# The first feed-forward of a mixer block begun row tile by row tile on four pairs of output blocks, in eight PSUM banks, with GpSimd taken out of the opening

## The chip, the cores and the metric

One NeuronCore of a Trainium2 chip runs the whole program. The metric is the device time of one execution in microseconds, lower being better; a verdict compares several executions of two kernels on the same chip.

## The reference

The block has a sequence of 512 rows and a width of 1024. A vector `c` gives nine modulation vectors of 1024 through one large matrix; the first feed-forward, the subject here, uses the first three (shift, scale, gate).

```python
cs  = silu(c)                                      # 1 x 1024
mod = (cs @ w_ada + b_ada).reshape(1, 3, 3, 1024)  # w_ada: 1024 x 9216
h   = rms_norm(x, norm_ffn1) * (1 + mod[:, 0, 1]) + mod[:, 0, 0]
gate, up = split(h @ w_ffn1_in, 2)                 # w_ffn1_in: 1024 x 5632
x   = x + 0.5 * mod[:, 0, 2] * ((silu(gate) * up) @ w_ffn1_out)
...                                                # token mixer, second feed-forward, final norm
```

All arrays are fp32.

## The kernel before, in words

Activations are held transposed: eight row tiles of 128 features by 512 sequence positions (`x[:, k]`, k = 0 to 7). A product in near-fp32 precision is made of three matmuls on fp32r operands: each operand is split into a rounded part and a remainder (`hh`/`hl` for the activations, `whi`/`wlo` for the weights), and `mm3` adds whi·hh, whi·hl and wlo·hh for every row tile k into one PSUM bank of 128 x 512. ScalarE makes the rounded part (a Copy, L226 for weights, L320 for activations), VectorE or GpSimd the remainder by a subtraction (L227, L321).

The opening, before the first feed-forward can run freely, goes so. SyncE loads `c` as one row, then `x`, `cols`, two constant matrices, and then the modulation matrix in 1 MB pieces (`adaw`, five buffers) and the first weights (`raw`, two buffers). `c` goes through Silu and is spread over the 128 partitions as `cs` by matmuls against a row of ones and two PSUM copies (L246 to L251). ScalarE squares the tiles of `x` (L291), VectorE adds them (L293), TensorE sums over partitions, GpSimd takes the power -0.5 (L308), TensorE spreads the result into a bank and ScalarE copies it to `rbs` (L405).

Then a loop over q = 0 to 3 (L409 to L418) takes two row tiles at a time: `ada(1, q)` and `ada(0, q)` compute scale and shift of tiles 2q and 2q + 1 by VectorE multiply-and-accumulate instructions (L260, 128 x 1024 each, four in a round); for q < 2 the weights of one pair of output blocks (gate and up block j = q, 1 MB) are split, with the remainder on GpSimd; GpSimd multiplies `x[:, k]` by `rbs` (L415), ScalarE applies scale and shift (L416) and rounds (L320), VectorE makes the remainder (L321).

`ffn` has 22 pairs of output blocks in two halves of 11, and an output product of eight blocks behind each half. Its first two pairs use four banks (`big`, `big`, `st`, `st`), the following ones the three `big` banks in turn; each pair is 48 matmuls, and then ScalarE and VectorE compute silu(gate)·up and split it. Beside it run 28 pieces of the remaining modulation work (`side`, 1 MB and two L260 instructions each), the first behind pair 2; their buffers lie where the opening's pool `p0` was.

Instructions are written in program order, but a planner sets the order on each engine and each queue from its own estimates of when operands and buffers are ready: an instruction whose inputs come late by the estimate is passed by later ones. Each engine then runs its list strictly in that order.

Of the kernel before, what the change touches and what calls it, by code (L numbers as in the profile page):

```python
# [17 lines left out]
P = 128  # L18
# [4 lines left out]
DFF = 2816  # L23
NJ = DFF // P
HJ = NJ // 2
H = 8
EPS = 1e-6
QS = float(P) ** -0.5
# [60 lines left out]
def layout(inputs):  # L89
    g = {k: np.asarray(v) for k, v in inputs.items()}  # L90

    def col(v):
        return v.reshape(-1, P).T

    def ktile(w):
        return w.reshape(-1, P, w.shape[1]).transpose(1, 0, 2)

    a = {}
    a["xT"] = ktile(g["x"][0].T)
    a["wada"] = g["w_ada"][0].T.reshape(36, 2, P, D).transpose(0, 2, 1, 3)  # L100
    a["crow"] = g["c"]
    cw = g["gdn_conv_w"][0].reshape(5, 24, P).transpose(2, 1, 0).reshape(P, 120)
    a["cols"] = np.concatenate([
        col(g["b_ada"][0]), col(g["norm_ffn1"][0]), col(g["norm_mix"][0]),
        col(g["norm_ffn2"][0]), col(g["norm_final"]), cw,
        col(g["mlstm_out_norm"][0]), col(g["gdn_out_norm"][0])], axis=1)
    mb, dt = g["mlstm_gate_bias"][0], g["gdn_dt_bias"][0]
    z = np.zeros(8, mb.dtype)
    a["rows"] = g["gdn_a_log"][0].reshape(1, 16)
    a["gbias"] = np.concatenate([mb[1], mb[3], dt[0], dt[1], mb[0], mb[2], z, z])[:, None]  # L110
    for n in (1, 2):
        wi = g[f"w_ffn{n}_in"][0].reshape(KO, P, 2, NJ, P)
        a[f"wi{n}"] = wi.transpose(3, 1, 0, 2, 4)
        wo = g[f"w_ffn{n}_out"][0].reshape(2, HJ, P, KO, P)
        a[f"wo{n}"] = wo.transpose(3, 0, 2, 1, 4)
    wk = ktile(g["w_in"][0])

    def blk(base, i):
        return wk[:, :, base + i * P: base + (i + 1) * P]

    def pair(b0, i0, b1, i1):
        return np.concatenate([blk(b0, i0), blk(b1, i1)], axis=2)

    gi = [MG + 8, MG + 24, GG, GG + 16, MG, MG + 16, GG + 8, GG + 24]
    a["wgate"] = np.concatenate([wk[:, :, b:b + 8] for b in gi] + [np.zeros((P, KO, 64), wk.dtype)], axis=2)
    a["wmqk"] = np.stack([pair(MQ, h, MK, h) for h in range(H)])
    a["wmv"] = np.stack([wk[:, 4 * kp:4 * kp + 4, MV + 512 * n: MV + 512 * (n + 1)]
                         for n in range(2) for kp in range(2)])
    a["wgkq"] = np.stack([pair(GK, h, GQ, h) for h in range(H)])
    for nm, b in (("wmo", MO), ("wgv", GV), ("wgz", GZ), ("wmm", MM), ("wmg", MGG)):  # L130
        a[nm] = np.stack([wk[:, :, b + 256 * i: b + 256 * (i + 1)] for i in range(4)])
    for nm, k in (("wbm", "w_branch_mlstm"), ("wbg", "w_branch_gdn"), ("wout", "w_out")):
        w = ktile(g[k][0])
        a[nm] = np.stack([w[:, :, 256 * i: 256 * (i + 1)] for i in range(4)])
    a["cst"] = _constants()
    return {k: np.ascontiguousarray(v) for k, v in a.items()}
# [25 lines left out]
def hybrid_block(ctx: ExitStack, tc: tile.TileContext, I, outT, dbg=None, upto=99):  # L162
# [21 lines left out]
    def sm():  # L184
        b = ps.tile([P, S], F32, tag="sm", name="psm", bufs=3)
        return b

    def mm(o, l, r, start=True, stop=True):
        pe.matmul(o, l, r, start=start, stop=stop)  # L189
# [7 lines left out]
    p0s = ExitStack()  # L197
    cs = p1.tile([P, D], F32, name="cs")
    p0 = Lines(p0s.enter_context(tc.tile_pool(name="p0", bufs=1, side="right")))
    crow = p0.tile([1, D], F32, name="crow")  # L200
    nc.sync.dma_start(crow, I["crow"])
    cstt = cst.tile([P, NK], F32, name="cstt")
    for q in range(4):
        nc.sync.dma_start(x[:, q * 2:(q + 1) * 2], I["xT"][:, q * 2:(q + 1) * 2])
    nc.sync.dma_start(cols, I["cols"])
    nc.sync.dma_start(cstt[:, 0:2 * P], I["cst"][:, 0:2 * P])
    C = {n: cstt[:, i * P:(i + 1) * P] for i, n in enumerate(KEPT)}
    one1 = C["ones"][:, 0:1]

    def colv(n):  # L210
        o, w = COL_OFF[n]
        return cols[:, o:o + w]
# [17 lines left out]
    def wk(src, c=256, lo=vec):  # L230
        hi, lo = wtile(src, KO * c, lo)
        return (hi[:, :KO * c].rearrange("p (k c) -> p k c", c=c),
                lo[:, :KO * c].rearrange("p (k c) -> p k c", c=c))
# [8 lines left out]
    modc = cst.tile([P, 72], F32, name="modc")  # L242
    scol = cst.tile([P, 24], F32, name="scol")
    ghalf = cst.tile([P, 16], F32, name="ghalf")
    orow = p0.tile([1, P], F32, name="orow")
    vec.memset(orow, 1.0)  # L246
    act.activation(crow, crow, AF.Silu)
    for q in range(2):
        pcs = sm()
        mm(pcs, orow, crow[:, q * S:(q + 1) * S])  # L250
        vec.tensor_copy(cs[:, q * S:(q + 1) * S], pcs)  # L251
    nrm = {0: "n1", 1: "nm", 2: "n2"}

    def ada(bk, q, tp, nb=2):
# [64 lines left out]
    def split(dst_h, dst_l, src):  # L319
        act.activation(dst_h, src, AF.Copy)  # L320
        vec.tensor_tensor(out=dst_l, in0=src, in1=dst_h.bitcast(F32), op=ALU.subtract)  # L321
# [20 lines left out]
    def ffn(x, hh, hl, gcol, wi, wo, tp, norm, side=(), pre=(), first=(ALL,), store=None):  # L342
        side, pre = list(side), list(pre)
        sq = {}
        for half in range(2):
            ah, al = [], []
            for jj in range(HJ):
                j = half * HJ + jj
                if j == 0:
                    w0 = pre or [wk(wi[i]) for i in range(2)]  # L350
                    p0 = [(big(), big()), (st2(), st2())]
                    for c, _ in first:
                        for (wh, wl), pp in zip(w0, p0):
                            for o, c0 in zip(pp, (0, P)):
                                mm3(o[:, c], lambda k: wh[:, k, c0:c0 + P], lambda k: wl[:, k, c0:c0 + P],
                                    lambda k: hh[:, k, c], lambda k: hl[:, k, c])
                if j < 2:
                    pg, pu = p0[j]
                else:
                    wh, wl = wk(wi[j])  # L360
                    pg, pu = big(), big()
                    for o, c0 in ((pg, 0), (pu, P)):
                        mm3(o, lambda k: wh[:, k, c0:c0 + P], lambda k: wl[:, k, c0:c0 + P],
                            lambda k: hh[:, k], lambda k: hl[:, k])
                sg = tp.tile([P, S], F32, tag="sg", name="sg", bufs=2)
                act.activation(sg, pg, AF.Silu)  # L366
                vec.tensor_tensor(out=sg, in0=sg, in1=pu, op=ALU.mult)  # L367
                a_h = tp.tile([P, S], F32R, tag="acth", name="acth", bufs=HJ + 2)
                a_l = tp.tile([P, S], F32R, tag="actl", name="actl", bufs=HJ + 2)
                split(a_h, a_l, sg)  # L370
                ah.append(a_h)
                al.append(a_l)
                if side and j > 1:
                    side.pop(0)()

            def out_block(o, wh, wl, c):
                po = big()
                mm3(po[:, c], lambda k: wh[:, k * P:(k + 1) * P], lambda k: wl[:, k * P:(k + 1) * P],
                    lambda k: ah[k][:, c], lambda k: al[k][:, c], n=HJ)
                vec.scalar_tensor_tensor(out=x[:, o, c], in0=po[:, c], scalar=gcol[:, o:o + 1], in1=x[:, o, c],  # L380
                                         op0=ALU.mult, op1=ALU.add)
                if half == 1:
                    sumsq(x, o, sq, tp, c)
                    if store is not None and c.stop == S:
                        nc.sync.dma_start(store[:, o], x[:, o])

            for o in range(KO - 2 * half):
                out_block(o, *wtile(wo[o, half], HJ * P), ALL[0])
                if half == 0 and side:
                    side.pop(0)()  # L390
        w2 = [wtile(wo[o, 1], HJ * P) for o in (KO - 2, KO - 1)]
        for c, ts in HALVES:
            for o, w in zip((KO - 2, KO - 1), w2):
                out_block(o, *w, c)
            norm(sq, c, ts)
        assert not side, len(side)
# [7 lines left out]
    rbs = p0.tile([P, S], F32, name="rbs")  # L404
    act.activation(rbs, rb, AF.Copy)  # L405
    hh, hl = new_h()
    pre = []
    for q in range(4):
        ada(1, q, p0, 5)  # L409
        ada(0, q, p0, 5)  # L410
        if q < 2:
            pre.append(wk(I["wi1"][q], lo=pool))
        for k in range(2 * q, 2 * q + 2):
            xn = p0.tile([P, S], F32, tag="xn", name="xn", bufs=4)
            pool.tensor_tensor(out=xn, in0=x[:, k], in1=rbs, op=ALU.mult)  # L415
            act.activation(xn, xn, AF.Identity, bias=modc[:, k:k + 1], scale=scol[:, k:k + 1])  # L416
            split(hh[:, k], hl[:, k], xn)
    p0s.close()  # L418
    pa1 = Lines(p1s.enter_context(tc.tile_pool(name="pa1", bufs=1, side="right")))
    gbias = cst.tile([64, 1], F32, name="gbias")  # L420
# [856 lines left out]
```

## Time and profile before

| | us |
|---|---|
| median of 3 runs | 1614.32 (1611.21, 1614.32, 1614.54) |
| the profiled execution | 1608.13 |
| its span, first to last instruction | 1606.3 |
| TensorE, granted clock over the span | 0.991 |

Engine names: PE is TensorE (PEld its weight loads), DVE VectorE, ACT ScalarE, POOL GpSimd, SP the queue that issues the DMAs. In a timeline row the first number is the start, the second the time to the end of the group of `xN` instructions; in brackets stands the idle time before it and what ended that. Durations of matmuls overlap, so the distance between starts is what one costs.

### The profile page before, as it was taken

The numbers are of one execution on the slowest core, as the hardware profiler recorded it, in microseconds if no ns is written. First come the engines' busy times: TensorE is split into PE (matmuls) and PEld (weight loads), VectorE is DVE, ScalarE is ACT, GpSimd is POOL, SyncE is SP. The second block draws the span as 40 slices with busy tenths as digits, with TensorE's granted clock in tenths as the row PEclk, the third lists the DMA queues.
The fourth block names the chain that finished last, engine by engine and source line by source line (L and its number), as shares of the span: only waits on it lengthen the run. The fifth ranks groups of instructions, "written<-read, shape, count | busy, mean of one in ns | idle before, by whom it ended". The sixth has DMA issues, their size and how long they took to land.

```text
span 1606.3 us, 20850 instructions
## 1 busy us (share of the span) xinstructions
PE 1553.8 (97%) x7944; PEld 1296.2 (81%) x7944; DVE 879.3 (55%) x1625; ACT 686.6 (43%) x1538; POOL 117.7 (7%) x121
## 2 busy tenths in 40 slices
PE   3999999999999999999999998999999999999997
PEld 2788888888878888888888886888889888888887
DVE  6878753333855555566666689346656433333333
ACT  3322122222526767595685732247623322123232
POOL 4100000000000000012111203500000000000000
PEclk9999999999999999999999998999999999999999
DMA  8577742223311111344544495676352222332122
GB/s 336 198 301 261 281 169 102 97 79 126 142 69 63 53 53 54 111 154 148 209 181 148 170 323 150 209 246 240 127 182 80 101 83 73 121 108 97 71 90 71
DMA packets 68613, 236.04 MB, mean 147 GB/s; under 512 B 23201, under 2 KB 25633, under 8 KB 50466
## 3 DMA queue, kind: packets, MB, share of 16 engines
q1 hardware_dynamic: 68514, 234.72, 41.2%
q8 instruction: 63, 1.03, 0.2%
q14 instruction: 36, 0.29, 0.1%
HBM read 199.04 MB, written 35.65 MB: 146 GB/s over the span
## 4 chain that ended last, share of the span: by engine, by line
PE 86%; DVE 8%; DMA 2%; ACT 1%; issue 1%; SPq 0%; POOL 0%; POOLq 0%; DVEq 0%; ACTq 0%
PE pbig L189 72%; PE pst L189 7%; PE psm L189 7%; DVE adaw L260 1%; DVE ot L1009 1%; DVE Wm L1011 1%; DVE wlo L227 1%; DMA vt<-vtd 1%; DVE hl L321 1%; PE pst L837 0%; DMA X<-xtd 0%; ACT whi L226 0%; DVE sqacc L293 0%; DMA raw<-in_wi 0%; PE pst L870 0%
## 5 line engine op out<-in xcount | busy, mean ns | idle before, releaser
L189 PE MATMUL pbig<-hh,whi 128*128 128x512 f32 (+1 forms) x1328 | 522.2, 394 | 8.4 <-ACT hh L320 8.4
L189 PE MATMUL pbig<-hh,wlo 128*128 128x512 f32 (+1 forms) x1328 | 519.5, 391 | 1.4 <-POOL wlo L227 1.4
L189 PE MATMUL pbig<-hl,whi 128*128 128x512 f32 (+1 forms) x1328 | 518.4, 391 | 2.5 <-DVE hl L321 2.4
L226 ACT ACTIVATE whi<-raw 128x1024 fp32r<-128x1024 f32 (+1 forms) x257 | 245.5, 991 | 461.9 <-PE pbig L189 388.0
L227 DVE TENSOR_TENSOR wlo<-raw,whi 128x1024 fp32r<-128x1024 f32 (+1 forms) x253 | 283.8, 1142 | 50.2 <-ACT whi L226 44.8
L189 PEld LDWEIGHTS pbig<-hh,whi 128*128 128x128 f32 x1328 | 251.1, 189 | 57.7 <-ACT hh L320 9.5
L189 PEld LDWEIGHTS pbig<-hl,whi 128*128 128x128 f32 x1328 | 251.2, 189 | 52.8 <-DVE hl L321 4.1
L189 PEld LDWEIGHTS pbig<-hh,wlo 128*128 128x128 f32 x1328 | 250.9, 189 | 51.3 <-POOL wlo L227 1.9
L367 DVE TENSOR_TENSOR sg<-sg,pbig 128x512 f32<-128x512 f32 x42 | 28.8, 687 | 245.5 <-PE pbig L189 245.5
L189 PE MATMUL pbig<-acth,whi 128*128 128x512 f32 (+1 forms) x396 | 146.1, 369 | 0.0
L189 PE MATMUL pbig<-acth,wlo 128*128 128x512 f32 (+1 forms) x396 | 145.6, 368 | 0.0
L189 PE MATMUL pbig<-actl,whi 128*128 128x512 f32 (+1 forms) x396 | 145.6, 368 | 0.0
L260 DVE SCALAR_TENSOR_TENSOR adaw<-adaw,cs 128x1024 f32<-128x1024 f32 x72 | 91.3, 1293 | 12.4 <-DMA adaw<-in_wada 12.3
L189 PEld LDWEIGHTS pbig<-acth,whi 128*128 128x128 f32 x396 | 74.5, 188 | 13.1
L189 PEld LDWEIGHTS pbig<-acth,wlo 128*128 128x128 f32 x396 | 74.5, 188 | 13.1
L189 PEld LDWEIGHTS pbig<-actl,whi 128*128 128x128 f32 x396 | 74.5, 188 | 13.0
L380 DVE SCALAR_TENSOR_TENSOR x<-pbig,ghalf,x 128x512 f32<-128x512 f32 (+1 forms) x36 | 24.8, 690 | 107.4 <-PE pbig L189 107.4
L830 DVE SCALAR_TENSOR_TENSOR cacc<-pbig,cols,cacc 128x510 f32<-128x510 f32 (+1 forms) x96 | 69.9, 745 | 24.5 <-ACT cacc L825 23.1
L366 ACT ACTIVATE sg<-pbig 128x512 f32<-128x512 f32 x42 | 25.1, 598 | 132.1 <-PE pbig L189 132.1
L308 POOL TENSOR_TENSOR rr<-ms,mhalf 128x2 f32<-128x2 f32 (+1 forms) x7 | 6.1, 876 | 928.3 <-DVE ms L305 734.9
L885 POOL TENSOR_SCALAR kd<-tt,ckd 128x128 f32<-128x128 f32 x64 | 46.0, 740 | 240.2 <-DVE ckd L881 156.6
L701 DVE TENSOR_TENSOR bd<-psm,negm 128x512 f32<-128x512 f32 x16 | 10.3, 685 | 38.8 <-PE psm L189 38.8
(338 smaller groups left out, 1985.5 us busy)
## 6 DMA issues: line engine op xcount, KB each, us to landing
raw<-in_wi SPq DMA_DIRECT2D x44, 1024.0 KB, 4.8
adaw<-in_wada SPq DMA_DIRECT2D x36, 1024.0 KB, 6.8
raw<-in_wo SPq DMA_DIRECT2D x32, 704.0 KB, 4.1
raw<-in_wmqk SPq DMA_DIRECT2D x8, 1024.0 KB, 4.8
raw<-in_wgkq SPq DMA_DIRECT2D x8, 1024.0 KB, 5.6
tad<-TA SPq DMA_DIRECT2D x8, 1024.0 KB, 4.5
raw<-in_wmv SPq DMA_DIRECT2D x4, 1024.0 KB, 4.8
raw<-in_wmo SPq DMA_DIRECT2D x4, 1024.0 KB, 4.8
```

The source lines that it names most:

```text
L189: pe.matmul(o, l, r, start=start, stop=stop)
L226: act.activation(hi[:, e], raw[:, e], AF.Copy)
L227: lo.tensor_tensor(out=wl[:, e], in0=raw[:, e], in1=hi[:, e].bitcast(F32), op=ALU.subtract)
L260: vec.scalar_tensor_tensor(out=raw[:, n], in0=raw[:, n], scalar=1.0, in1=cs, op0=ALU.mult, op1=ALU.mult, accum_out=acc[:, n:n + 1])
L321: vec.tensor_tensor(out=dst_l, in0=src, in1=dst_h.bitcast(F32), op=ALU.subtract)
L366: act.activation(sg, pg, AF.Silu)
L367: vec.tensor_tensor(out=sg, in0=sg, in1=pu, op=ALU.mult)
L380: vec.scalar_tensor_tensor(out=x[:, o, c], in0=po[:, c], scalar=gcol[:, o:o + 1], in1=x[:, o, c], op0=ALU.mult, op1=ALU.add)
L830: vec.scalar_tensor_tensor(out=acc[:, o], in0=pz[:, i], scalar=w[:, j:j + 1], in1=acc[:, o], op0=ALU.mult, op1=ALU.add)
L885: pool.tensor_scalar(out=kd[:, d, t], in0=ktt[:, t], scalar1=ckd[:, t, d, h:h + 1], scalar2=None, op0=ALU.mult)
L1009: vec.tensor_tensor(out=ov, in0=Um[:, d, r, j:j + 1].to_broadcast([P, n, 32 - n]), in1=Wm[:, d, j:j + 1, c].to_broadcast([P, n, 32 - n]), ...
L1011: vec.tensor_tensor(out=Wm[:, d, r, c], in0=Wm[:, d, r, c], in1=ov, op=ALU.subtract)
```

## The change

`c` is loaded by one DMA into all 128 partitions and goes through Silu there; the matmuls and copies that spread it are gone. The constants are loaded ahead of `cols`. The weights of the first four pairs are laid out anew on the way in (`wis`: for every row tile, the four pairs' gate and up columns, 0.5 MB a tile), and the loop runs over the eight row tiles: load scale and shift pieces (0.5 MB each) and the weights of the tile, split the weights (remainder on VectorE), compute scale and shift of that one tile, modulate with `mod_k` (two VectorE instructions around one of ScalarE), and issue the tile's 24 matmuls into eight banks. `ffn` takes the eight banks as its pairs 0 to 3 and loads weights from pair 4 on. The power -0.5 stays on GpSimd.

```diff
 NS = 4
@@ layout
+        if n == 1:
+            a["wis"] = a["wi1"][:NS].reshape(NS, P, 4, 2, 2, P).transpose(2, 3, 1, 0, 4, 5).reshape(4, 2, P, NS * 2 * P)
+            a["wi1"] = a["wi1"][NS:]
@@ hybrid_block
-    crow = p0.tile([1, D], F32, name="crow")
-    nc.sync.dma_start(crow, I["crow"])
+    nc.sync.dma_start(cs, I["crow"].partition_broadcast(P))
     cstt = cst.tile([P, NK], F32, name="cstt")
     for q in range(4):
         nc.sync.dma_start(x[:, q * 2:(q + 1) * 2], I["xT"][:, q * 2:(q + 1) * 2])
+    nc.sync.dma_start(cstt[:, 0:2 * P], I["cst"][:, 0:2 * P])
     nc.sync.dma_start(cols, I["cols"])
-    nc.sync.dma_start(cstt[:, 0:2 * P], I["cst"][:, 0:2 * P])
...
-    orow = p0.tile([1, P], F32, name="orow")
-    vec.memset(orow, 1.0)
-    act.activation(crow, crow, AF.Silu)
-    for q in range(2):
-        pcs = sm()
-        mm(pcs, orow, crow[:, q * S:(q + 1) * S])
-        vec.tensor_copy(cs[:, q * S:(q + 1) * S], pcs)
+    act.activation(cs, cs, AF.Silu)
@@ ffn
-                if j == 0:
-                    w0 = pre or [wk(wi[i]) for i in range(2)]
+                if j == 0 and not pre:
+                    w0 = [wk(wi[i]) for i in range(2)]
...
-                if j < 2:
+                if j < len(pre):
+                    pg, pu = pre[j]
+                elif j < 2:
                     pg, pu = p0[j]
                 else:
-                    wh, wl = wk(wi[j])
+                    wh, wl = wk(wi[j - len(pre)])
@@ the opening's loop
-    pre = []
-    for q in range(4):
-        ada(1, q, p0, 5)
-        ada(0, q, p0, 5)
-        if q < 2:
-            pre.append(wk(I["wi1"][q], lo=pool))
-        for k in range(2 * q, 2 * q + 2):
-            xn = p0.tile([P, S], F32, tag="xn", name="xn", bufs=4)
-            pool.tensor_tensor(out=xn, in0=x[:, k], in1=rbs, op=ALU.mult)
-            act.activation(xn, xn, AF.Identity, bias=modc[:, k:k + 1], scale=scol[:, k:k + 1])
-            split(hh[:, k], hl[:, k], xn)
+    pre = [(big(), big()), (big(), st2()), (st2(), sm()), (sm(), sm())]
+    for k in range(KO):
+        k2, half = k // 2, k % 2
+        raw = p0.tile([P, 2, D], F32, tag="adaw", name="adaw", bufs=5)
+        for n in (1, 0):
+            nc.sync.dma_start(raw[:, n], I["wada"][n * 4 + k2][:, half])
+        if half == 0:
+            wr = W.tile([P, 2, NS, 2, P], F32, tag="raw", name="raw", bufs=2)
+            wh = W.tile([P, 2, NS, 2, P], F32R, tag="whi", name="whi")
+            wl = W.tile([P, 2, NS, 2, P], F32R, tag="wlo", name="wlo")
+        nc.sync.dma_start(wr[:, half].rearrange("p j c n -> p (j c n)"), I["wis"][k2, half])
+        act.activation(wh[:, half], wr[:, half], AF.Copy)
+        acc = p0.tile([P, 2], F32, tag="adacc", name="adacc", bufs=4)
+        for n in (1, 0):
+            vec.scalar_tensor_tensor(out=raw[:, n], in0=raw[:, n], scalar=1.0, in1=cs, op0=ALU.mult, op1=ALU.mult,
+                                     accum_out=acc[:, n:n + 1])
+        vec.tensor_tensor(out=modc[:, k:k + 9:8], in0=acc, in1=colv("b_ada")[:, k:k + 9:8], op=ALU.add)
+        vec.scalar_tensor_tensor(out=scol[:, k:k + 1], in0=modc[:, 8 + k:9 + k], scalar=1.0,
+                                 in1=colv("n1")[:, k:k + 1], op0=ALU.add, op1=ALU.mult)
+        mod_k(x, 0, k, rbs if k else rb, hh, hl, p0)
+        vec.tensor_tensor(out=wl[:, half], in0=wr[:, half], in1=wh[:, half].bitcast(F32), op=ALU.subtract)
+        for j in range(NS):
+            for o, c in zip(pre[j], range(2)):
+                mm(o, wh[:, half, j, c], hh[:, k], start=(k == 0), stop=False)
+                mm(o, wh[:, half, j, c], hl[:, k], start=False, stop=False)
+                mm(o, wl[:, half, j, c], hh[:, k], start=False, stop=(k == KO - 1))
```

## Rows read from the trace of the kernel before

**Rows 1.** Page: busy time by engine; the chain that ended last, by engine.
```profile
PE 1553.8 (97%) x7944; PEld 1296.2 (81%) x7944; DVE 879.3 (55%) x1625; ACT 686.6 (43%) x1538; POOL 117.7 (7%) x121
...
PE 86%; DVE 8%; DMA 2%; ACT 1%; issue 1%; SPq 0%; POOL 0%; POOLq 0%; DVEq 0%; ACTq 0%
```
**Rows 2.** Chain of waits, first 250 us: start, length, what.
```profile
24.57 3.30 DVE adaw L260 x2
27.86 2.75 DVE hl L321
...
41.50 3.32 DVE adaw L260 x2
...
65.42 184.69 PE pbig L189 x807
```
**Rows 3.** Windows of the opening: PE, PEld, DVE, ACT, POOL busy, clock, DMA, GB/s.
```profile
20.00:30.00 10.00, 3.24 (x5) 1.41 (x5) 6.64 (x5) 4.56 (x6) 10.00 (x6) 1.00 1.00 424
30.00:40.00 10.00, 4.80 (x10) 3.32 (x11) 6.55 (x10) 3.25 (x5) 5.37 (x4) 1.00 0.59 197
40.00:50.00 10.00, 9.44 (x31) 6.78 (x30) 9.96 (x11) 1.31 (x2) 8.16 (x4) 1.00 0.46 173
```
**Rows 4.** Timeline: what leads to the first row tile, and the next VectorE instructions.
```profile
14.07 0.16 DVE L302 TENSOR_SCALAR ms<-psm 128x4 f32<-128x4 f32 x1 [1.96 <-PE psm L189]
...
16.29 2.08 PE L189 MATMUL psm<-cstt,rr 128*128 128x128 f32 x8 [2.25 <-POOL rr L308]
...
16.44 0.08 DVE L260 DVE_READ_ACCUMULATOR adaw<-adaw,cs 128x1 f32 x1
...
16.82 1.22 DVE L260 SCALAR_TENSOR_TENSOR adaw<-adaw,cs 128x1024 f32<-128x1024 f32 x1
...
17.97 1.22 DVE L260 SCALAR_TENSOR_TENSOR adaw<-adaw,cs 128x1024 f32<-128x1024 f32 x1
...
23.98 6.08 POOL L227 TENSOR_TENSOR wlo<-raw,whi 128x1024 fp32r<-128x1024 f32 x2
...
24.49 3.37 DVE L260 SCALAR_TENSOR_TENSOR adaw<-adaw,cs 128x1024 f32<-128x1024 f32 x1
```
**Rows 5.** Instructions by form: mod_k's two and the weight remainder, 300 to 420 us.
```profile
L227 DVE TENSOR_TENSOR wlo<-raw,whi 128x1024 fp32r<-128x1024 f32 x17 | 20.5, 1223 | 1.5 <-ACT whi L226 0.9
L326 DVE SCALAR_TENSOR_TENSOR xr<-x,scol,psm 128x256 f32<-128x256 f32 x14 | 6.2, 475 | 2.1 <-PE psm L189 2.1
L329 DVE SCALAR_TENSOR_TENSOR hl<-xr,modc,hh 128x256 fp32r<-128x256 f32 x12 | 5.4, 479 | 0.2 <-ACT hh L328 0.2
...
L321 DVE TENSOR_TENSOR actl<-sg,acth 128x512 fp32r<-128x512 f32 x5 | 3.4, 684 | 0.0
```
**Rows 6.** Timeline of PE, 23 to 70 us.
```profile
23.73 0.80 PE L189 MATMUL pbig<-hh,whi 128*128 128x512 f32 x1 [5.36 <-ACT hh L320]
...
38.56 0.80 PE L189 MATMUL pst<-hh,whi 128*128 128x512 f32 x1 [4.54 <-ACT whi L226]
...
43.73 0.63 PE L189 MATMUL pbig<-hl,whi 128*128 128x512 f32 x1
44.16 0.63 PE L189 MATMUL pbig<-hh,wlo 128*128 128x512 f32 x1
44.59 0.61 PE L189 MATMUL pbig<-hl,whi 128*128 128x512 f32 x1
...
47.37 0.39 PE L189 MATMUL pbig<-hh,wlo 128*128 128x512 f32 x1
47.59 0.40 PE L189 MATMUL pst<-hh,wlo 128*128 128x512 f32 x1
...
65.25 0.39 PE L189 MATMUL pbig<-hh,whi 128*128 128x512 f32 x1
...
69.79 0.39 PE L189 MATMUL pbig<-hh,wlo 128*128 128x512 f32 x1
```
**Rows 7.** DMA by fortieths of the first 70 us, GB/s (1.75 us each).
```profile
GB/s 2 215 398 377 366 437 431 403 440 435 421 421 445 417 412 445 435 234 0 117 421 110 344 323 5 75 370 155 0 0 0 9 0 0 0 98 407 431 337 407
```
**Rows 8.** Timeline of the queue SP: the next weights and the first side pieces.
```profile
34.99 9.10 SPq L217 DMA_DIRECT2D raw<-in_wi  x2
61.08 0.80 SPq L256 DMA_DIRECT2D adaw<-in_wada  x2
```
**Rows 9.** Waits of the queue SP, 0 to 110 us: us in total, times, longest.
```profile
SPq L256 <- DVE hl L321: 16.8, 1, 16.8
```
**Rows 10.** Windows of the side pieces' VectorE instructions: busy (count), clock, DMA share, GB/s.
```profile
180.00:220.00 40.00, 15.74 (x28) 1.00 0.73 263
220.00:260.00 40.00, 0.00 (x0) 1.00 0.29 106
```

More of the change, by code (lines that the diff above doesn't have):

```diff
@@ L25 @@
 HJ = NJ // 2
+NS = 4
 H = 8
```

## The prediction

> **What bounds the kernel now.** I read the page first. TensorE is busy 97% of the span and has 86% of the chain that ended last [rows 1], so the time is the length of TensorE's stream; a change can only pay by taking a hole or slow matmuls out of that stream. The chain of waits shows where one lies: from 65.42 us on it is TensorE without a break (807 matmuls in one piece), but up to there it goes through VectorE, tile by tile [rows 2]. The windows say the same: between 20 and 40 us TensorE is busy 8.0 of 20 us, while GpSimd is busy 15.4 [rows 3]. And the timeline of TensorE shows a second loss: matmuls of 512 columns start 0.43 us apart up to 44.59 and 0.23 us apart later (47.37 to 47.59) [rows 6]. By 512 columns per distance these are its two levels, 1.2 and 2.4 GHz, although the windows give a granted clock of 1.00 throughout [rows 3]; I go by the distances.
>
> So the opening does little in 65 us. Two pairs are 2 x 2 blocks x 8 tiles x 3 = 96 matmuls, and pair 2 begins at 65.25. A full-speed matmul costs (69.79 - 65.25) / 20 = 0.227 us [rows 6]: 96 are 21.8 us. The other 43 us are waiting or the slow clock.
>
> **The measuring point.** The change has 192 matmuls (four pairs) behind it when pair 4 begins. Before, pair 4 would begin at 65.25 + 96 x 0.227 = 87.0 us. If the changed kernel begins pair 4 at T, the gain is 87.0 - T, since all behind it is TensorE's stream in both.
>
> **The change, part by part.**
>
> *Start of the first tile.* Spreading `c` by DMA puts 0.5 MB ahead of `x`; at the 366 to 398 GB/s of the slices in which `x` comes (4 KB rows) that is 1.3 us [rows 7]. Silu over 128 partitions costs ScalarE about what one row of 1024 did, before the squares and while `x` still flies. Against it, two copies of 0.68 us leave VectorE's chain of additions. The trace has no broadcast of this size: bounds are 1.9 us gained (the copies and the gaps about them, `x` undelayed) and 4 us lost (the broadcast three times slower than `x`); I take 0.3 lost, the copies nearly paying for the delay, and keep the ends. The path to the bank with the norm's factor stays: ms at 14.07, GpSimd's power, eight matmuls that end at 18.37 [rows 4]. VectorE does tile 0's two modulation instructions in that gap. Then xr, hh, hl. The trace has xr and hl at 128 x 256, 0.475 us [rows 5]; at 512 columns they lie between 0.68 (the plain subtraction of that size) and 0.95 (twice 0.475); I take 0.74, nearer to the plain row. With 0.62 for ScalarE: first matmul 18.4 + 0.74 + 0.62 = 19.8, steady from about 20.6. Before it was 23.73, and the second had to wait.
>
> *VectorE per tile.* Two L260 at a distance of 1.15 us (16.82 to 17.97), 0.38 for modc and scol (16.44 to 16.82) [rows 4], xr and hl 0.67 each (0.74 less the 0.07 by which neighbours overlap), the weight remainder 1.15: 2.30 + 0.38 + 1.34 + 1.15 = 5.2 us. While hh is made, 0.6 us can stay open unless the planner puts the weight remainder there: 5.2 to 5.9 us. VectorE gains the remainders of four pairs (eight of 1.15) and xr, but GpSimd's company goes: one L260 beside GpSimd's subtraction took 3.37 us instead of 1.22, and the subtraction itself 6.08 for two [rows 4]; the chain shows it again at 27.86 and 41.50 [rows 2].
>
> *TensorE per tile.* 24 matmuls: 5.45 us at full speed, 10.3 at 0.43. Since 10.3 is well over VectorE's 5.2 to 5.9, tile 0 makes TensorE work without a break from 20.6 on. Before, the distances shortened after 6.0 us of work with one break of 0.4 us (38.56 to 44.59) [rows 6]. I take the same 6.0: slow until 26.6, some 15 matmuls done, 177 left at 0.227 = 40.2, end 66.8. VectorE has tile 7 ready at 21.8 + 7 x 5.2 = 58 (5.9: 63), TensorE needs it at 61: TensorE leads, with the slow case 2 us behind. For this and the 0.3 above I add 1.5: T = 68.3.
>
> *Loads.* 24 pieces of 0.5 MB (two of modulation, one of weights per tile) are 12.6 MB; at 376 GB/s that is 33.5 us behind `x`'s end near 10.4, so 4.2 us per tile against VectorE's 5.2: the queue leads. Five `adaw` buffers allow it; the third weight buffer waits for tile 1's remainder (near 27), with tile 4 wanted at 42. 24 issues of at most 0.5 us are 12 us of SP. If loads fell behind, each us would be lost in full; the margin at tile 7 is over 5 us.
>
> *Hand-over to pair 4.* Before, weights of pairs 2 and 3 were issued ahead of the side pieces, which waited 16.8 us for the opening's pool [rows 8, 9]; I expect the same for pair 4. Its raw buffer comes free with tile 5's remainder (near 48), its rounded buffer when TensorE leaves tile 5 (near 57); 2 us of ScalarE and 2.3 of VectorE end near 62, six us before T. Its bank is free after a Silu of 0.6 us on pair 0, whose last matmul is 18 matmuls (4.1 us) before T. So nothing is lost; if pair 4's load stood behind two side pieces, it would come near 69 and cost 1 to 5 us. The side pieces end by 220 us, and their instructions fill 40% of VectorE until then [rows 10], so a shorter feed-forward does not run into them.
>
> *Sum.* 87.0 - 68.3 = 18.7 us. The profiled execution took 1608.13 (span 1606.3 and 1.8 around it): 1589.4. It is the fastest of four known times; from the median, 1614.32, it is 1595.6, from the mean of the four, 1612.05, 1593.3. I say 1594.5.
>
> **Rivals.**
>
> *VectorE leads.* Each engine runs a fixed list, planned on estimates. If xr cost 0.95, hh's gap stayed open and ScalarE sat behind a weight rounding whose buffer TensorE still holds, a tile costs 6.5 to 7.5 us: T = 21.8 + 7 x 7 + 5.4 = 76, gain 11: 1603 (1600 to 1606). For it: VectorE is 99.6% busy from 40 to 50 us [rows 3]. Against: without GpSimd its instructions are 1.2 us, not 3.4.
>
> *The clock does not hold while eight banks are cycled.* The matmuls change bank every third instruction, and every tile touches all eight. If TensorE fell back to 0.43 us between tiles, 177 matmuls would cost up to 0.2 us more each: 35 us, T = 103, 16 us slower, 1630; the break-even is 18.7 / 0.2 = 94 slow matmuls, about half. At half of them slow the kernel is unchanged, 1613. Against it: in the trace of before the matmuls change between four banks of two pairs at 0.22 us (47.37 `pbig`, 47.59 `pst`) [rows 6], and short holes did not bring the long distance back. Eight banks appear nowhere.
>
> The Trainium skill, TensorE: Matmul & The Clock Gate, section "A second HAM failure mode: psum-queue depth-cycling", says that cycling PSUM banks in each iteration made TensorE idle briefly so often that its clock went back and forth. By that rule the time would be the one of the rival just priced; the trace with four banks does not bear it out.
>
> *Nothing comes of it.* The first tile starts late (4 us of broadcast), VectorE leads, and the hand-over costs 5: gain 19 - 4 - 8 - 5 = 2 us, 1612.
>
> **How the numbers follow.** The forecast has 0.74, VectorE leading 0.15, the clock 0.06 (slower in 0.05), nothing 0.05. About 0.2%, 3.2 us, is what a measurement of this kernel can tell from no change. Faster: 0.74 + 0.15 = 0.89; same 0.05; slower 0.06. Range: downward the best start (1.9 us) and the fast profile as a base, 1587; upward to the middle of VectorE leading, 1604. Both sides of that leave out under 0.2.
>
> **What would show it.** Right: GpSimd's only work in the opening is the power; L260 at 1.22 us throughout; the first tile's matmul near 20 us; distances of 0.43 turning to 0.23 before 32 us; 192 matmuls over at 66 to 71 us and pair 4 without a hole; the rest of the chain unchanged. Wrong: holes of TensorE in front of each tile, ended by hl or wlo (VectorE leads); long distances after 35 us (clock); a hole before pair 4 ended by its weights; pair 4 beginning after 84 us.

## The result, and the profile after

| us | before | after |
|---|---|---|
| median (lowest to highest) | 1613.04 (1611.21 to 1614.54) | 1593.57 (1590.96 to 1595.03) |
| the profiled execution | 1608.13 | 1594.81 |
| its span | 1606.3 | 1593.0 |
| pair 4 begins (before: worked out as 87.0) | 87.0 | 68.55 |

The ratio is 0.9878 with an interval of 0.9858 to 0.9898: 19.5 us faster, where 18.7 us and 1594.5 were forecast. Four runs stand behind each median.

The page of the changed kernel, busy time and the chain by engine. GpSimd lost 25 us of work, and VectorE's share of the chain fell from 8% to 6% [rows 1]:

```profile
PE 1546.9 (97%) x7940; PEld 1295.3 (81%) x7940; DVE 877.3 (55%) x1638; ACT 682.9 (43%) x1530; POOL 92.5 (6%) x109
...
PE 87%; DVE 6%; ACT 2%; DMA 2%; issue 1%; POOL 1%; SPq 1%; POOLq 0%; DVEq 0%; ACTq 0%
```

The windows of the opening, columns as in [rows 3]. TensorE is busy 18.1 of the 20 us in which it was busy 8.0; GpSimd does nothing:

```profile
20.00:30.00 10.00, 8.10 (x23) 6.44 (x24) 9.38 (x15) 4.46 (x6) 0.00 (x0) 1.00 0.95 381
30.00:40.00 10.00, 10.00 (x46) 8.29 (x45) 9.93 (x19) 2.74 (x3) 0.00 (x0) 1.00 0.94 336
40.00:50.00 10.00, 10.00 (x45) 8.05 (x45) 9.93 (x19) 3.47 (x4) 0.00 (x0) 1.00 0.68 234
```

The chain of waits from its start, the answer to [rows 2]. From 21.90 us on it is TensorE alone, in pieces of different banks; in before that began at 59.68. The last piece shown is pair 4 and what follows; a piece of the chain starts 0.16 us behind its first matmul:

```profile
1.17 5.55 DMA x<-in_xT
...
15.61 1.93 POOL rr L305
...
20.29 0.94 ACT whi L417
21.23 0.62 ACT hh L325
21.90 1.65 PE pbig L193 x3
...
68.71 231.38 PE pbig L193 x1013
```

The timeline of PE, the answer to [rows 6]. The distance between starts is 0.43 us up to 27.61 and 0.23 us from 28.02, and stays there through all eight tiles; pair 4 begins at 68.55 without idle time before it:

```profile
21.90 1.65 PE L193 MATMUL pbig<-hh,whi 128*128 128x512 f32 x3 [2.24 <-ACT hh L325]
...
27.18 0.63 PE L193 MATMUL pst<-hl,whi 128*128 128x512 f32 x1
27.61 0.58 PE L193 MATMUL pst<-hh,wlo 128*128 128x512 f32 x1
28.02 0.39 PE L193 MATMUL pst<-hl,whi 128*128 128x512 f32 x1
28.25 0.40 PE L193 MATMUL pst<-hh,wlo 128*128 128x512 f32 x1
...
52.22 0.39 PE L193 MATMUL pbig<-hh,whi 128*128 128x512 f32 x1
...
68.55 0.39 PE L193 MATMUL pbig<-hh,whi 128*128 128x512 f32 x1
```

The timeline of VectorE, the answer to [rows 4, 5]. No modulation instruction is longer than 1.22 us; xr and hl cost 0.75 at 512 columns:

```profile
15.37 0.16 DVE L299 TENSOR_SCALAR ms<-psm 128x4 f32<-128x4 f32 x1 [1.96 <-PE psm L193]
15.45 1.22 DVE L420 SCALAR_TENSOR_TENSOR adaw<-adaw,cs 128x1024 f32<-128x1024 f32 x1
...
20.32 0.75 DVE L323 SCALAR_TENSOR_TENSOR xr<-x,scol,psm 128x512 f32<-128x512 f32 x1 [2.12 <-ACT rbs L404]
21.27 1.23 DVE L426 TENSOR_TENSOR wlo<-raw,whi 128x1024 fp32r<-128x1024 f32 x1 [0.20 <-ACT whi L417]
22.41 0.74 DVE L326 SCALAR_TENSOR_TENSOR hl<-xr,modc,hh 128x512 fp32r<-128x512 f32 x1
...
51.50 0.75 DVE L326 SCALAR_TENSOR_TENSOR hl<-xr,modc,hh 128x512 fp32r<-128x512 f32 x1
```

The queue SP, the answer to [rows 8]: pair 4's weights are issued from 47.08 on, the first side piece at 59.63.

```profile
47.08 10.28 SPq L220 DMA_DIRECT2D raw<-in_wi  x2
59.63 0.80 SPq L253 DMA_DIRECT2D adaw<-in_wada  x2
```

**A landmark.** One VectorE instruction in the token mixer (MR from cmx, BR) starts at 450.46 us in before and at 432.01 in after (first line before, second after): 18.45 us, what the beginning of pair 4 says too.

```profile
450.46 0.28 DVE L577 TENSOR_SCALAR MR<-cmx,BR 8x128 f32<-8x128 f32 x1
432.01 0.28 DVE L591 TENSOR_SCALAR MR<-cmx,BR 8x128 f32<-8x128 f32 x1
```

In the experiments I use it beside pair 4, since it also sees holes in the feed-forward. The two profiled executions differ by only 13.3 us (1606.3 less 1593.0), because more is lost behind the landmark: TensorE has the same hole of 1.95 us in both, and in after the granted clock is lower in the 5 us from the landmark's waits on (0.72, before 0.92), which takes 1.6 us of the lead. One window of after, and the same of before:

```profile
432.00:437.00 5.00, 3.17 (x12) 2.51 (x13) 4.69 (x18) 0.00 (x0) 0.00 (x0) 0.72 0.40 167
```

```profile
450.50:455.50 5.00, 3.22 (x20) 2.84 (x20) 4.70 (x18) 0.00 (x0) 0.00 (x0) 0.92 0.39 164
```

Another 1.8 us goes by 927 us, about one of them in a longer wait for a DMA (6.7 us instead of 5.7), and 1.7 in small pieces up to the end. Before's profiled run is faster than each of its other runs; the medians, 19.5 us apart, agree with the landmark.

### The profile page after: what moved, and what is told of

Same layout as the page of the kernel before. It is cut to its first block, busy times and chain, and to the rows that moved or that the text cites. A ratio compares the mean times of both kernels' runs of the same rounds, so it can differ in the third digit from the quotient of the medians.

```text
span 1593.0 us, 20834 instructions
## 1 busy us (share of the span) xinstructions
PE 1546.9 (97%) x7940; PEld 1295.3 (81%) x7940; DVE 877.3 (55%) x1638; ACT 682.9 (43%) x1530; POOL 92.5 (6%) x109
## 4 chain that ended last, share of the span: by engine, by line
PE 87%; DVE 6%; ACT 2%; DMA 2%; issue 1%; POOL 1%; SPq 1%; POOLq 0%; DVEq 0%; ACTq 0%
PE pbig L193 70%; PE psm L193 8%; PE pst L193 7%; DVE wlo L230 1%; DVE Wm L1025 1%; DVE ot L1023 1%; DMA X<-xtd 0%; PE pst L851 0%; POOL kd L899 0%; DMA raw<-in_wgkq 0%; DMA vt<-vtd 0%; SPq L934 0%; DMA x<-in_xT 0%; DVE sqacc L290 0%; POOL rr L305 0%
## 5 line engine op out<-in xcount | busy, mean ns | idle before, releaser
L193 PE MATMUL pbig<-hh,whi 128*128 128x512 f32 (+1 forms) x1304 | 511.1, 393 | 2.2 <-ACT hh L325 2.2
L193 PE MATMUL pbig<-hh,wlo 128*128 128x512 f32 (+1 forms) x1304 | 509.0, 390 | 0.0
L193 PE MATMUL pbig<-hl,whi 128*128 128x512 f32 (+1 forms) x1304 | 507.5, 389 | 0.0
L229 ACT ACTIVATE whi<-raw 128x1024 fp32r<-128x1024 f32 (+1 forms) x249 | 237.5, 990 | 451.9 <-PE pbig L193 366.1
L230 DVE TENSOR_TENSOR wlo<-raw,whi 128x1024 fp32r<-128x1024 f32 (+1 forms) x249 | 279.3, 1142 | 51.1 <-ACT whi L229 46.1
L193 PEld LDWEIGHTS pbig<-hh,whi 128*128 128x128 f32 x1304 | 245.8, 189 | 49.3 <-ACT hh L325 2.5
L193 PEld LDWEIGHTS pbig<-hl,whi 128*128 128x128 f32 x1304 | 246.4, 189 | 48.1 <-DVE hl L326 0.3
L193 PEld LDWEIGHTS pbig<-hh,wlo 128*128 128x128 f32 x1304 | 245.8, 189 | 48.6
L257 DVE SCALAR_TENSOR_TENSOR adaw<-adaw,cs 128x1024 f32<-128x1024 f32 x56 | 66.9, 1221 | 13.7 <-DMA adaw<-in_wada 13.7
L325 ACT ACTIVATE hh<-xr,modc 128x256 fp32r<-128x256 f32 (+1 forms) x40 | 20.5, 545 | 41.3 <-DVE xr L323 41.3
```

Source lines behind the costliest of these rows:

```text
L229: act.activation(hi[:, e], raw[:, e], AF.Copy)
L230: lo.tensor_tensor(out=wl[:, e], in0=raw[:, e], in1=hi[:, e].bitcast(F32), op=ALU.subtract)
L257: vec.scalar_tensor_tensor(out=raw[:, n], in0=raw[:, n], scalar=1.0, in1=cs, op0=ALU.mult, op1=ALU.mult, accum_out=acc[:, n:n + 1])
L325: act.activation(hh[:, k, c], xr, AF.Identity, bias=b)
```

## The experiments

Each kernel ran beside the kernel before on one chip: the first four (median of before 1613.93), the next four (1612.08), the last three (1611.91).

| | median | ratio (interval) | first matmul behind the opening's pairs | landmark |
|---|---|---|---|---|
| two pairs | 1602.56 | 0.9931 (0.9916 to 0.9945) | pair 2: 56.76 | 441.98 |
| three pairs | 1598.53 | 0.9900 (0.9883 to 0.9916) | pair 3: 61.76 | 436.53 |
| remainder on GpSimd | 1600.94 | 0.9922 (0.9907 to 0.9937) | pair 4: 73.74 | 438.81 |
| before without GpSimd | 1600.97 | 0.9926 (0.9911 to 0.9940) | pair 2: 55.63 | 440.86 |
| `c` behind `x` | 1591.91 | 0.9875 (0.9860 to 0.9890) | pair 4: 66.92 | 430.38 |
| warm | 1590.44 | 0.9870 (0.9856 to 0.9885) | pair 4: 67.81 | 432.29 |
| both | 1588.37 | 0.9853 (0.9836 to 0.9869) | pair 4: 65.63 | 430.93 |
| both, one tile ahead | 1587.77 | 0.9852 (0.9837 to 0.9867) | pair 4: 65.48 | 429.11 |
| GpSimd work added | 1609.18 | 0.9993 (0.9975 to 1.0011) | pair 4: 83.76 | 447.69 |
| changed kernel again | 1592.88 | 0.9877 (0.9855 to 0.9899) | pair 4: 68.65 | 432.10 |
| three side buffers | 1588.51 | 0.9852 (0.9832 to 0.9871) | pair 4: 66.00 | 429.45 |

### How many pairs

Two pairs, as in before, but in the new order:

```diff
-NS = 4
+NS = 2
-    pre = [(big(), big()), (big(), st2()), (st2(), sm()), (sm(), sm())]
+    pre = [(big(), big()), (st2(), st2())]
```

> The changed kernel with two pairs of output blocks in the opening instead of four, all else the same. Theory (the gain is TensorE work put beside VectorE's tiles): VectorE needs 5.2 - 0.6 = 4.6 to 4.7 us a tile, tile 7 is ready near 56, twelve matmuls more: pair 2 begins at 58 to 59 instead of 65.25, 6 to 8 us faster than the kernel before. Rival 1 (taking GpSimd out makes the gain): as good as with four pairs, 16 us or more faster. Rival 2 (the row-tile order alone does it): likewise.

Three pairs:

```diff
-NS = 4
+NS = 3
-    pre = [(big(), big()), (big(), st2()), (st2(), sm()), (sm(), sm())]
+    pre = [(big(), big()), (big(), st2()), (st2(), sm())]
```

> The changed kernel with three pairs in the opening. Theory: VectorE needs 4.9 us a tile and leads (18 matmuls are 4.1 us): pair 3 begins near 61.5, against 65.25 + 48 x 0.227 = 76.1 before: 14 to 15 us faster than before, between two pairs and four. Rival (TensorE alone leads): 144 matmuls end near 57.5, as much as 18 us faster, no less than with four.

The chain's piece that begins behind the opening's pairs, for two and for three:

```profile
56.92 243.17 PE pbig L193 x1065
```

```profile
61.92 76.17 PE pbig L193 x336
```

Pair 2 begins 8.5 us earlier than in before (65.25), and the landmark moves by as much; with three pairs its lead is 13.9, with four 18.45. So the third pair is worth 5.5 and the fourth 4.5 us, and the rivals of the two-pair run, by which two pairs would do as well as four, fall. TensorE's waits in front of tiles go the same way: 8.5 us with two pairs (7.4 for hh, 1.1 for hl), 5.5 with three, 2.2 with four, of which all are the wait for the first tile. A pair added here is 48 matmuls that fill time in which TensorE waited for VectorE; with four there is none left to fill. The waits are 3.0 of the third pair's 5.5 us and 3.3 of the fourth's 4.5. Much of what is missing for the third is the clock: with two pairs the first tile runs at 0.43 us a matmul to its end, and behind the waits ahead of and in tile 2 (1.2 and 0.5 us) that distance comes back from 34.78 to 37.75, which it does not with three or four.

### GpSimd back, and GpSimd out alone

The changed kernel with the weight remainder on GpSimd, as in before:

```diff
-        vec.tensor_tensor(out=wl[:, half], in0=wr[:, half], in1=wh[:, half].bitcast(F32), op=ALU.subtract)
+        pool.tensor_tensor(out=wl[:, half], in0=wr[:, half], in1=wh[:, half].bitcast(F32), op=ALU.subtract)
```

> The changed kernel with the weights' remainder (one instruction of 128 x 1024 a tile) on GpSimd instead of VectorE. Theory (GpSimd's work stretches VectorE's beside it): in the kernel before 24.5 us of GpSimd in the opening went with some 12 us of stretch on VectorE, 0.5 each; eight subtractions of 2.8 us would cost VectorE 11 us and save it 9: pair 4 begins 1 to 4 us later than at 68.55. Rival (VectorE leads and GpSimd does it no harm): VectorE needs 4.0 us a tile, TensorE alone leads, pair 4 begins at 67 or earlier.

Pair 4 begins 5.2 us later, and a hole of 1.4 us follows at 86.60; the landmark's lead falls by 6.8, to 11.7. The direction was right, the size larger, although VectorE had eight instructions of 1.22 us less to do. Its timeline and GpSimd's in one tile show why:

```profile
31.30 1.22 DVE L420 SCALAR_TENSOR_TENSOR adaw<-adaw,cs 128x1024 f32<-128x1024 f32 x1
...
32.57 2.23 DVE L422 TENSOR_TENSOR modc<-adacc,cols 128x2 f32<-128x2 f32 x1
```

```profile
31.36 3.42 POOL L426 TENSOR_TENSOR wlo<-raw,whi 128x1024 fp32r<-128x1024 f32 x1 [4.06 <-ACT whi L417]
```

An addition of 128 x 2, 0.16 us in after, takes 2.23 and ends (34.80) with GpSimd's subtraction (34.78). The subtraction in its turn was ready at 31.36, while VectorE's instruction ran to 32.45; the 2.3 us from there are its own. In these rows they do not run side by side: they take turns, whole instruction by whole instruction.

The other side, before with only GpSimd's two jobs put on VectorE (two pairs and the loop over q stay):

```diff
-            pre.append(wk(I["wi1"][q], lo=pool))
+            pre.append(wk(I["wi1"][q]))
-            xn = p0.tile([P, S], F32, tag="xn", name="xn", bufs=4)
-            pool.tensor_tensor(out=xn, in0=x[:, k], in1=rbs, op=ALU.mult)
-            act.activation(xn, xn, AF.Identity, bias=modc[:, k:k + 1], scale=scol[:, k:k + 1])
-            split(hh[:, k], hl[:, k], xn)
+            mod_k(x, 0, k, rbs if k else rb, hh, hl, p0)
```

> The kernel before with GpSimd's two jobs in the opening given to VectorE (weight remainders of two pairs, and the modulation by the changed kernel's mod_k), the loop over q and the two pairs kept. Theory: VectorE's stretch of some 12 us goes, 10 us of work come: pair 2 begins 1 to 5 us earlier than 65.25, 1 to 5 us faster than before. Rival 1 (taking GpSimd out makes the gain): 12 us or more faster.

My theory fell here, and the rival's 12 us did not come either: pair 2 begins at 55.63, 9.6 us earlier, and the landmark leads by 9.6. More than half of the whole gain comes without row tiles, without more banks. The sum on VectorE nearly closes. From ms (14.07) to the end of the last hl (60.95) it took 46.9 us in before; now 14.13 to 51.46, 37.3. In before, three waits for hh fill 8.9 of that, by VectorE's list of waits up to 66 us (total, times, longest):

```profile
DVE hl L321 <- ACT hh L320: 8.9, 3, 3.4
```

This kernel has none of them, but a new one, for ScalarE's copy of the norm's factor:

```profile
DVE xr L326 <- ACT rbs L405: 2.1, 1, 2.1
```

And ten instructions were stretched: three of L260 by 5.4 us together (3.37, 3.38 and 2.29 instead of 1.22), four hl by 4.2 (0.86, 2.82, 1.50 and 1.76 instead of 0.68), three modc by 2.9 (1.11 to 1.13 instead of 0.16): 12.5. What VectorE takes over is eight xr of 0.67 and four remainders of 1.15, 10.0. So 46.9 - 8.9 + 2.1 - 12.5 + 10.0 = 37.6, measured 37.3. The work moved in cost VectorE 2.5 us less than GpSimd's company did; the greater part, 6.8 us, are waits. And these were mostly not GpSimd's. In before the way to hh goes through ScalarE twice, and at the first two of the three waits a rounding of weights stands between; this is the second:

```profile
36.75 0.81 ACT L416 ACTIVATE xn<-xn,modc,scol 128x512 f32<-128x512 f32 x1 [11.71 <-DVE modc L262]
37.47 1.99 ACT L226 ACTIVATE whi<-raw 128x1024 fp32r<-128x1024 f32 x2
39.36 0.61 ACT L320 ACTIVATE hh<-xn 128x512 fp32r<-128x512 f32 x1
```

The third, of 2.17 us, ends at 59.66, when GpSimd has been idle since 48.78. The edit changes two things, who does the work and how often the way to hh goes through ScalarE (mod_k: once), and no run takes them apart; 6.8 and 2.5 are read from the rows.

### What the start costs

The broadcast of `c` issued behind `x`, its Silu behind the squares:

```diff
-    nc.sync.dma_start(cs, I["crow"].partition_broadcast(P))
     for q in range(4):
         nc.sync.dma_start(x[:, q * 2:(q + 1) * 2], I["xT"][:, q * 2:(q + 1) * 2])
+    nc.sync.dma_start(cs, I["crow"].partition_broadcast(P))
...
-    act.activation(cs, cs, AF.Silu)
...
+    act.activation(cs, cs, AF.Silu)     # behind the loop over the squares
```

> The changed kernel with the broadcast of c issued behind x instead of ahead of it, and its Silu behind the squares. Theory (the broadcast costs the start what its 0.5 MB take): ms comes at 14.1 instead of 15.37, the first tile's matmul near 20.6 instead of 21.90, and pair 4 begins 1.0 to 1.5 us earlier than at 68.55. Rival (the modulation pieces' arrival sets the pace): ms comes earlier, but pair 4 begins at 68.5 as before.

The norm's input moves to 13.72 and pair 4 to 66.92: 1.6 us, at the landmark as well. That is what spreading `c` ahead of `x` costs; the Silu that moved with it is not in it, since in after ScalarE was through with it and waited 0.50 us more for `x`.

```profile
13.72 0.16 DVE L298 TENSOR_SCALAR ms<-psm 128x4 f32<-128x4 f32 x1 [1.96 <-PE psm L193]
```

The slow spell: 53 matmuls on zeros, into a spare bank, written as 36 at the start, 8 between the norm's two groups and 9 ahead of the first tile (the planner ran 43 of them ahead of the norm, then 2 and 8).

```diff
+    wz = p0.tile([P, S], BF16, name="wz")
+    vec.memset(wz, 0.0)
+    junk = sm()
+    def warm(n):
+        for _ in range(n):
+            mm(junk, wz[:, 0:P], wz)
+    warm(36)
...
-    rb = rms_bcast(sq, p1, fold=True)
+    rb = rms_bcast(sq, p1, fold=True, mid=warm)     # warm(8) between its two groups
+    warm(9)
```

> The changed kernel with 53 matmuls of zeros put on TensorE while it waits for x, the norm and the first tile, so that the distances are 0.23 us from the first tile on. Theory of the forecast (TensorE alone leads): some 15 slow matmuls at 0.2 us each are saved, pair 4 begins near 65.5, 3 us earlier. Rival, read from the trace after (VectorE's list is just in time for tiles 3 and 5: hl of tile 5 ends at 52.2, TensorE comes to it at 52.2): the saved time is waited for at tile 5, 52.2 + 3 x 5.45 = 68.6, pair 4 begins at 68.0 to 68.6.

The first tile's matmuls are 0.23 us apart from 21.12 on; without the 14 slow ones, 0.2 us each, 2.8 us should have been gained. But pair 4 comes only 0.74 us earlier, and the whole of that is the norm (its matmuls shorter, ms at 14.59 instead of 15.37). What the clock gave came back as waiting, 1.9 us of it in two holes ahead of tiles 2 and 3, the rest in longer distances next to them; here is the second:

```profile
40.13 0.96 PE L193 MATMUL pbig<-hh,whi 128*128 128x512 f32 x3 [1.40 <-ACT hh L336]
```

So the rival of this run held, with the holes three tiles earlier than it said: TensorE was not alone in the lead, VectorE's list was just in time. In after, tile 5 begins at 52.22 and its hl runs from 51.50 to 52.25. The landmark does not move against after (432.29), a hole of 0.8 us later in the feed-forward included, and the ratio, 0.9870, lies inside the interval of the change.

Both together (28, 8 and 9 warm matmuls):

> Both edits: c behind x and TensorE busy ahead of the first tile. VectorE just in time: pair 4 begins at 67 to 67.3, no better than c behind x alone. TensorE alone leads: 64 to 64.5.

Pair 4 begins at 65.63, 2.9 us earlier, more than one edit alone and between the two times expected. Of that 1.6 us are lost near 197 us, where the side pieces' loads had become the chain, with two buffers that VectorE gives back late:

```profile
187.02 7.74 DMA adaw<-in_wada
...
196.68 1.14 DVE wlo L230
```

```profile
PE pbig L193 <- DVE wlo L230: 1.6, 1, 1.6
```

Scale and shift of the next tile computed ahead of modulating this one, on top of both:

```diff
+    adak(0)                     # loads, L420s, modc and scol of a tile
     for k in range(KO):
...
+        if k + 1 < KO:
+            adak(k + 1)
         mod_k(x, 0, k, rbs if k else rb, hh, hl, p0)
```

> As both edits, and the scale and shift of tile k + 1 written ahead of tile k's modulation, so that the planner may put them into VectorE's 2 us of waiting for the norm's factor. VectorE just in time: if the order on VectorE improves, up to 2 us earlier than with both edits, pair 4 begins at 65 to 67; if the planner leaves the 2 us open, 67 to 68.

Pair 4 begins at 65.48, hardly earlier, but the holes ahead of tiles are gone and so is the one at 197: the landmark is at 429.11, 2.9 us ahead of after. The medians of the two, 1588.37 and 1587.77, can't be told apart. The first tile is slow again for its first matmuls (eight starts, 0.43 to 0.48 us apart; with both edits nine), so neither has the whole of the warm start.

### GpSimd's company priced by itself

The changed kernel, with one subtraction per tile on GpSimd whose result nobody uses:

```diff
         act.activation(wh[:, half], wr[:, half], AF.Copy)
+        jk = p0.tile([P, NS, 2, P], F32, tag="jk0", name="jk0", bufs=1)
+        pool.tensor_tensor(out=jk, in0=wr[:, half], in1=wh[:, half].bitcast(F32), op=ALU.subtract)
```

> The changed kernel with one more GpSimd subtraction of 128 x 1024 per tile, whose output nobody reads; VectorE's own work is unchanged. Theory (VectorE and GpSimd take turns here: in the kernel with GpSimd back, VectorE's modc of 128 x 2 took 2.24 us and ended with GpSimd's instruction): each costs VectorE some 2.2 us, a tile takes 7.4 us instead of 5.2, tile 7 is ready near 75 and pair 4 begins 10 to 13 us later than at 68.55. Rival (the stretch of half a microsecond per microsecond that I took at first): 6.3 to 6.7 us a tile, 4 to 7 us later. Rival (none of it costs anything once VectorE has its own work): 0 to 1 us.

Pair 4 begins at 83.76, 15.2 us later, more than the 10 to 13 expected, and most of the whole gain is gone: the median is that of before within what can be told (0.9993). Each of the eight subtractions stretches VectorE's list once, whichever instruction it meets:

```profile
22.46 2.86 DVE L326 SCALAR_TENSOR_TENSOR hl<-xr,modc,hh 128x512 fp32r<-128x512 f32 x1
25.25 3.41 DVE L422 SCALAR_TENSOR_TENSOR adaw<-adaw,cs 128x1024 f32<-128x1024 f32 x1
...
42.31 3.41 DVE L428 TENSOR_TENSOR wlo<-raw,whi 128x1024 fp32r<-128x1024 f32 x1
45.65 2.30 DVE L424 TENSOR_TENSOR modc<-adacc,cols 128x2 f32<-128x2 f32 x1
```

2.86 instead of 0.74, 3.41 instead of 1.22 and 2.30 instead of 0.16 are 2.1 to 2.2 us a time, eight times 17.5 us, and VectorE's last hl ends 17.4 us later (77.02, in after 59.60). Of that 15.2 us reach pair 4: TensorE's waits for hh and hl are 11.6 us longer, and the rest are matmuls at 0.43 us behind the two longest waits (2.1 and 5.8 us), where the granted clock reads lower too (0.83 from 30 to 40 us, 0.70 from 50 to 60):

```profile
PE pbig L193 <- ACT hh L325: 12.4, 5, 5.8
```

The Trainium skill, SBUF — State Buffer, section "Who interferes with whom", says that a VectorE instruction with two inputs in SBUF and a GpSimd one that reads SBUF contend for a shared port, and that this is an exclusive lock: the second to issue blocks fully until the first is done. The rows above agree; the instructions stretched have two SBUF inputs each. No experiment here set out to try one with a single input.

### The control, and a third side buffer

The changed kernel again, unaltered, beside the last two:

> The changed kernel as it is, on the same chip as the version below, to compare the two. Expected at its ratio to the kernel before, 0.988, 1592 to 1594 us.

It gives 1592.88 (1591.21 to 1595.42) and the landmark at 432.10.

The version with one tile ahead, with three side buffers for two:

```diff
-        [lambda b=b, q=q: ada(b, q, pa1) for b in (2, 4, 3, 5, 7, 6, 8) for q in range(4)], pre, store=xd)
+        [lambda b=b, q=q: ada(b, q, pa1, 3) for b in (2, 4, 3, 5, 7, 6, 8) for q in range(4)], pre, store=xd)
```

> c behind x, TensorE kept busy, scale and shift one tile ahead (the version of e8), and three buffers instead of two for the side pieces beside the first feed-forward. In the kernel with both edits a chain of side loads (7 to 8 us each to landing) ends in a hole of 1.6 us near 197, by a weight remainder that stands behind a side piece on VectorE. Theory: with three buffers no such hole can come from two buffers; pair 4 begins near 65.5 as in e8 and the lead of 3 us over the changed kernel is kept to the end of the feed-forward: 1589 us or less on a chip on which the changed kernel takes 1592 to 1593. Rival: the order of loads alone sets it, and 3 us at the opening are lost again in the feed-forward.

VectorE's waits for side loads between 100 and 230 us fall from 14.1 to 1.1 us, and nothing comes of it: 1588.51 (1586.60 to 1589.50), landmark 429.45, since TensorE had no hole there any more. It is 4.4 us faster than the control beside it, 2.7 of it at the landmark. Both edits, one tile ahead and the third buffer are about 1588 us each, against 1593 of the change and 1612 of before; which of the three is best can't be told.

## Why the prediction was right

- *What bounds it.* Right: the time is TensorE's stream, and holes and slow matmuls taken from its first 65 us came off the end one for one (18.45 us at pair 4, 18.45 at the landmark).
- *Start of the first tile.* Too early: 21.90 instead of 19.8. I took 0.3 us for spreading `c` and kept 4 as the worst end; it is 1.3 at ms and, by the run with `c` behind `x`, 1.6 at pair 4. Of the rest, 0.6 us is ScalarE's copy of the bank to rbs (19.69): I had let xr begin when the bank was full, but it waits for that copy and begins at 20.32. The chain shows the weight rounding (0.94 us) ahead of hh, but it cost next to nothing: xr itself ran to 21.07, and hh began at 21.13.
- *Slow clock.* Right to a tenth: 6.1 us from 21.90 to 28.02, 14 matmuls; then 178 at 0.2277 us, 40.53, which ends at 68.55. I had 6.0, 15 and 177. That the length came out so close is luck in part: in the run with three pairs the same spell ended after 3.1 us (22.07 to 25.21), and why is open. The margin of 1.5 us that I had added, for the start and for VectorE close behind, was used up by the start; without it the forecast of pair 4 would have been 66.8, so 68.3 against 68.55 is luck as well.
- *VectorE per tile.* Right for each instruction (1.22, 0.75, 0.75) and for the gap behind the first xr, into which the planner put the remainder; tile 7 is ready at 59.60, where 58 was forecast. Wrong in "TensorE leads": the warm run shows the two level, and had the first tile been fast, nothing more would have come.
- *Loads and hand-over.* Right: no wait of TensorE between 60 and 380 us, pair 4's weights issued ahead of the side pieces.
- *VectorE leads* (1603): it does not come true, but it was nearer than I thought. *The clock with eight banks* (1630): falls, 0.23 us from 28.02 on; eight banks cycled without holes did not bring 0.43 back. The rule of the Trainium skill cited beside it is not borne out in this kernel. *Nothing comes of it* (1612): of the broadcast's 4 us only 1.3 to 1.6 were there, nothing of the rest.
- *What I did not see.* I forecast one sum and never split it. By the runs, 9.6 of the 18.45 us come with GpSimd's two jobs moved to VectorE; the new order with two pairs and the broadcast take 1.1 back (8.5), and if the broadcast costs its 1.6 us there too, the order by itself gives 0.5; the third and fourth pair bring 5.5 and 4.5. The stretched instructions stood in [rows 4], and I used them as a remark; the waits for hh, the greater part of the 9.6, I did not price at all. In the changed kernel GpSimd's blocking is shown by itself: 6.8 us at the landmark for the remainder put back, 15.2 at pair 4 for eight subtractions added.

## What to carry to other kernels

Read long instructions against short ones of the same form: here a 128 x 2 addition that took 2.2 us was waiting for another engine inside its own row, where no list of waits shows it. A job moved from GpSimd to a VectorE that is already the bound can still make that faster, if GpSimd's instruction blocks VectorE for longer than VectorE needs for the job (here 2.2 us against 1.15). Look at what else such a move changes: here it also shortened the way through ScalarE, and by the rows that was worth more. And when one engine is made faster, ask which is just behind: here the clock's 2.8 us came back as waiting at once.

## What was not expected of the hardware

GpSimd's subtraction of 128 x 1024 blocked VectorE for 2.1 to 2.2 us in the runs with it back or added, whatever VectorE's instruction cost (0.16, 0.74 or 1.22 us alone). The granted clock reads 1.00 in the window from 20 to 30 us, in which most matmuls of the first tile are 0.43 us apart, the lower level; the column does not show this spell, the distances do.
